# All five engines keep the written order in both attention stages, and the planner's estimate follows

## The chip, the core and the metric

The kernel runs on one core of a Trainium2 chip. The metric is device time in microseconds (us), the median of three runs. The engines are TensorE (PE; its weight loads are listed apart as PEld), VectorE (DVE), ScalarE (ACT), GpSimd (POOL) and SyncE (SP), which issues the DMAs.

## What is computed

One inference step of a two-layer decoder trunk, for a prompt of 1024 tokens and 8 samples of 4 new tokens each (32 more columns, 1056 in all), with model width 1024.

- Layer 0: stick-breaking attention with 8 heads of 64 beside a gated linear recurrence (RG-LRU); both outputs go through one output projection. Then an MLP with squared ReLU and width 4096.
- Layer 1: dilated sliding-window attention with 16 heads, three window branches merged by their softmax denominators, with a relative bias. Then the same kind of MLP, and a final RMS norm.
- The samples attend to a paged cache (layer 0) and to a window buffer (layer 1).

```python
z = einsum('bqhd,bkhd->bhqk', qb, k) * scale + bias          # layer 0
sp = where(mask, softplus(z), 0)
rest = cumsum(sp, reverse=True) - sp
w = where(mask, exp(log_sigmoid(z) - rest), 0)
o = einsum('bhqk,bkhd->bqhd', w, v)
...
p = exp(logits - m)                                           # layer 1, each branch
o = einsum('gnhqk,gnkhd->gnqhd', p, vb) / p.sum(-1)
```

## The kernel before

Activations lie transposed (features on partitions). For precision every matmul operand is split into a high and a low part, and a product takes three matmuls (high by high, high by low, low by high; `mm3`). So each tile that PE reads is made by a pair: ACT copies the high part, DVE or POOL subtracts it for the low part.

**The stages in order:** RG-LRU of layer 0 (to about 212 us), attention of layer 0 (212 to 688), first MLP (688 to 1512, with the sample caches of layer 1 prepared beside it), attention of layer 1 (1512 to 2266), last MLP.

**Inside an attention stage** heads are handled in pairs (4 pairs in layer 0, 8 in layer 1). Python generators each emit a piece of work and yield what they wait for: `heads` (scores, transposes, weighted values), `projections` (q, k and v of the next pair, 24 matmuls of 352 columns for each third of a tile, in two PSUM accumulators `mm`), `sb_samples` or `dl_samples`, and `early_out` (the first part of the output projection) beside the last pairs. `interleave` (L934) picks the next piece among those whose inputs the planner holds to be ready, by fixed weights. Each call of `interleave` covers one pair. `split_pair` (L732), called before it, plans the eight splits of the new pair (four of q, four of k) with `after`, 2000 columns apart: each is an ACT copy, then on DVE a second copy (q) or a subtraction (k), then for q a subtraction on POOL; in layer 1 two of the four k subtractions are on POOL. `dl_samples` has 16 small ACT copies `qw` per pair.

**The planner** is `Clock` (L60). It counts in columns (2400 to a us) and holds for each tile when it is written and last read. `Timed` (L128) wraps the engines' calls and prices each with a constant plus nanoseconds per element; `passed` (L189) does so for PE. An engine in `order` is counted first in, first out; for the others `fit` (L105) puts an operation into the first hole after its inputs are there, also ahead of operations that were emitted earlier. A `Later` (made by `after`, L259) is emitted when PE's planned time reaches its due time; if its inputs are planned over 200 columns late, it is put off (`events`, L194). A weight tile's split is such a `Later`, due 14000 columns after its load was emitted (`load` in `projections`, L709). So the planner's estimate sets the order of emission of every engine, PE and the DMA queue included.

**The order in which the engines really run** is fixed when the program is built. `manual` (L955) names the engines that keep the order of emission, before the change PE, SP and POOL. For ACT and DVE the framework's scheduler makes the order: by its own estimate of durations it lets an operation that it holds to be ready pass one that waits. In the first MLP (`first_mlp`, L1254) all five engines keep the order of emission already. On the chip each engine then works through its list.

All operations of DVE, ACT, POOL and SP show line L138 (the wrapper), matmuls L209, transposes L215. Tiles: `u` are work tiles (transposed weights, high and low), `tr`, `mm`, `pv` PSUM tiles, `f` the scan's tile, `sa` and `sb` scores, `mx` row maxima and sums, `qa`, `ka` (first head of a pair), `qb`, `kb` (second head) split queries and keys, `ql` the low queries, `ws` raw weights, `w` split weights.

Of the kernel before, what the change touches and what calls it, by code (L numbers as in the profile page):

```python
# [12 lines left out]
R = mybir.dt.float32r  # L13
# [3 lines left out]
PSUM = bass.MemoryType.PSUM  # L17
# [3 lines left out]
SEQ = 1024  # L21
NS = 32
NT = SEQ + NS
CW = NT // 3
# [12 lines left out]
def f32(ap):  # L37
    return ap.bitcast(F)
# [21 lines left out]
class Clock:  # L60
# [12 lines left out]
    def __getattr__(self, n):  # L73
        return getattr(self.nc, n)
# [51 lines left out]


class Timed:  # L128
    NS = {"scalar": (100, 0.82), "vector": (70, 1.04), "gpsimd": (100, 2.2), "sync": (0, 0)}

    def __init__(self, clock, e, engine):
        self.clock, self.e, self.engine = clock, e, engine
# [1 line left out]
    def __getattr__(self, n):  # L134
        f = getattr(self.engine, n)

        def call(*args, **kw):
            r = f(*args, **kw)  # L138
            aps = [a for a in list(args) + list(kw.values()) if hasattr(a, "name") and hasattr(a, "shape")]
            outs = aps[:1] + ([kw["accum_out"]] if "accum_out" in kw else [])  # L140
            if self.e == "sync":
                o = aps[0] if aps[0].space != DRAM else aps[1]
                cost = int(np.prod(o.shape)) * 4 / 360 * 2.4
                outs = [a for a in outs if a.space != DRAM]
                ins = [a for a in aps[1:] if a.space != DRAM]
            else:
                a, b = Timed.NS[self.e]
                cost = (a + b * int(np.prod(aps[0].shape[1:]))) * 2.4
                ins = aps[1:]
            self.clock.run(self.e, cost, outs, ins)  # L150
            return r
        call.timed = True
        return call
# [18 lines left out]
class Trunk:  # L172
# [35 lines left out]
    def mm(self, out, w, x, start, stop):  # L208
        self.nc.tensor.matmul(out, w, x, start=start, stop=stop)  # L209
        n = int(np.prod(x.shape[1:]))  # L210
        m = int(np.prod(w.shape[1:]))
        self.passed(max(n, 2 * m) if x.dtype == R else max(4 * n, 4 * m), [out], [w, x])

    def tr(self, out, x, ident):
        self.nc.tensor.transpose(out, x, ident)  # L215
# [126 lines left out]
    def mm3(self, ps, terms):  # L342
        n = len(terms)
        for i, (wh, wl, xh, xl) in enumerate(terms):
            mm = self.mm
            mm(ps, wh, xh, start=i == 0, stop=False)
            mm(ps, wh, xl, start=False, stop=False)
            mm(ps, wl, xh, start=False, stop=i == n - 1)
            if i < n - 1:
                yield 0, 0  # L350
# [31 lines left out]
    def norm_finish(self, st):  # L382
# [4 lines left out]
        def sums():  # L387
            ps = self.tr_ps([128, 9])
            for t in range(9):
                n = 128 if t < 8 else NS  # L390
                self.mm(ps[:n, t:t + 1], acc[:, t * 128:t * 128 + n], self.ones[:, 0:1],
# [6 lines left out]
    def spread_rstd(self, r, rstd):  # L398

        nc = self.nc  # L400
        for c in range(3):
            pb = self.tr_ps([128, 384])
            w = 0
            for t in range(3 * c, 3 * c + 3):
                n = 128 if t < 8 else NS
                self.mm(pb[:, w:w + n], r[:n, t:t + 1].to_broadcast([n, 128]),
# [4 lines left out]
    def rsqrt(self, ps, last=True):  # L411
# [6 lines left out]
        if last:  # L418
            nc.vector.memset(m[:, k:], 1.0)
            nc.vector.tensor_scalar(m[:NS, k:], ps[:NS, k:], 1.0 / D, EPS, op0=OP.mult, op1=OP.add)  # L420
        nc.scalar.activation(t, m, AF.Sqrt)
# [531 lines left out]
            e[2] += self.work - c0  # L953

    def manual(self):  # L955
        self.nc.order.add("gpsimd")
        return self.tc.manual_schedule(engines={mybir.EngineType.PE, mybir.EngineType.SP, mybir.EngineType.Pool, })

    def heads(self, pairs, q_step, k_step, v_step, T, far, done, lag):

# [293 lines left out]
    def first_mlp(self, st, rstd, w1, w2, h, nx):  # L1254
        nc, hp = self.nc, self.hp
        todo = self.caches(hp)
        raw, parts = {}, {}

        def load(u):
            g, x = divmod(u, 8)  # L1260
            if x < 4:
                c0 = (g * 4 + x) * 128
                raw[u] = self.raw_w(w1[:, :, c0:c0 + 128], 8, 128)
            else:
                raw[u] = self.raw_w(w2[:, g * 4:g * 4 + 4, (x - 4) * 256:(x - 3) * 256], 4, 256)

        def cut(u, half):
            if u >= 64:
                return
            if half == 0:  # L1270
                parts[u] = self.parts_w(*raw[u].shape[1:], *((hp, 2) if u % 3 == 2 else ()))
            (a, b), kb = parts[u], raw[u].shape[1]
            c = slice(0, kb // 2) if half == 0 else slice(kb // 2, kb)
            nc.scalar.activation(a[:, c], raw[u][:, c], AF.Copy)
            if half:
                nc.gpsimd.tensor_sub(b, raw.pop(u), f32(a))

        load(0)
        load(1)
        cut(0, 0)  # L1280
        cut(0, 1)
        load(2)
        cut(1, 0)
        cut(1, 1)
        load(3)
        next(todo)
        with self.tc.manual_schedule(engines={getattr(mybir.EngineType, e) for e in
                                              ("PE", "SP", "Pool", "Activation", "DVE")}):
            for u in range(64):
                g, x = divmod(u, 8)  # L1290
                if u + 4 < 64:
                    load(u + 4)
                if x == 0:
                    th, tl = ([hp.tile([128, NT], R, name=self.nm(t), tag=t, bufs=4) for _ in range(4)]
                              for t in ("th", "tl"))
                w = parts.pop(u)
                n = 0
                if x < 4:
                    for c in range(3):
                        s = slice(c * CW, (c + 1) * CW)  # L1300
                        ps = self.mm_ps([128, CW])
                        for _ in self.mm3(ps, [(w[0][:, k], w[1][:, k], st["xh"][k][:, s], st["xl"][k][:, s])
                                               for k in range(8)]):
                            pass
                        for t in st["ready"]:
                            t.run()
                        t = hp.tile([128, CW], F, name=self.nm("t"), tag="t", bufs=3)
                        q = hp.tile([128, CW], F, name=self.nm("t2"), tag="t2", bufs=3)
                        nc.vector.scalar_tensor_tensor(t, ps, 0.0, rstd[:, s], op0=OP.max, op1=OP.mult)
                        nc.scalar.activation(q, t, AF.Square)  # L1310
                        nc.scalar.activation(th[x][:, s], q, AF.Copy)
                        next(todo, None)
                        nc.vector.tensor_sub(tl[x][:, s], q, f32(th[x][:, s]))
                        next(todo, None)
                        if c < 2:
                            cut(u + 2, c)
                    continue
                step = self.norm_done(h, self.g[:, 1], nx) if g == 7 else None

                def done(m, s):  # L1320
                    nonlocal n
                    if step:
                        step(m, s)
                        if s.stop == NT:
                            nc.sync.dma_start(self.hs[1][m], h[m])
                    next(todo, None)
                    if n in (1, 3):
                        cut(u + 2, n // 2)
                    n += 1
                if u == 63:  # L1330
                    w1c = self.i["w_in_c"][0].rearrange("(k p) f -> p k f", p=128)
                    first = self.load_w(w1c[:, :, :128], 8, 128)
                    nx["w"] = first, self.after(14000, self.split_w, *first, need=first[:1], made=first[1:])
                m = 2 * (x - 4)
                for _ in self.contract(w, (m, m + 1), range(4), th, tl, h, done):
                    pass
            for _ in todo:
                pass
        self.norm_finish(nx)
# [763 lines left out]
```

## Time and profile before

| | us |
|---|---|
| median of 3 runs (lowest, highest) | 3074.31 (3070.54, 3074.38) |
| profiled execution, its own time | 3073.03 |
| its span, first to last instruction | 3071.3 |
| PE busy | 2874.8 (94%) |
| DVE busy | 1711.0 (56%) |
| ACT busy | 1258.4 (41%) |
| POOL busy | 978.9 (32%) |

Busy time is a mean over stages with different limits, and a busy PE is not PE at its peak. The view by stretches of time gives, for each stretch, the busy time of every engine with its number of instructions, the granted PE clock (1.00 is 2.4 GHz) and the load of the DMA engines. The views of waits name, for each engine, what ended its idle time.

### The profile page before, as it was taken

The page shows a single profiled execution, that of the slowest core. Times are in us where ns is not written, and L with a number is a line of the kernel's source. Part 1 is how long each engine was busy: PE and PEld are TensorE (multiplying, and loading weights), DVE is VectorE, ACT ScalarE, POOL GpSimd, SP SyncE. Part 2 cuts the span into 40 slices and gives each one's busy share as a digit, 9 for nine tenths or more (in the row PEclk, how much of TensorE's full clock was granted, in tenths as well). Part 3 has the DMA queues.
Part 4 walks back from the last instruction along what each step waited for, and adds up shares of the span by engine and source line. Part 5 has one row for each costly group of instructions (what it writes and reads, how often), then busy time and mean ns, then how long its engine had stood idle before and what let it go on. Part 6 is the DMA issues. An engine that isn't in the chain of part 4 may idle for free.

```text
span 3071.3 us, 49475 instructions
## 1 busy us (share of the span) xinstructions
PE 2874.8 (94%) x18608; PEld 2757.7 (90%) x18608; DVE 1711.0 (56%) x3657; ACT 1258.4 (41%) x2505; POOL 978.9 (32%) x613
## 2 busy tenths in 40 slices
PE   7878889979999999999999989998989999999998
PEld 7778878849999999999988888897889999999998
DVE  6868887875444444433467777766673333333335
ACT  4446666654333333333344555544452222122222
POOL 2436552443333333332412222222231122121222
PEclk9889999979999999999999999998999999999999
DMA  5111127574877777761365544555631111111111
GB/s 171 42 44 34 42 86 222 166 240 133 256 246 250 251 253 251 258 206 42 120 190 187 191 148 160 188 170 191 220 119 49 48 49 42 49 43 48 49 35 64
DMA packets 366728, 426.18 MB, mean 139 GB/s; under 512 B 23878, under 2 KB 292822, under 8 KB 366488
## 3 DMA queue, kind: packets, MB, share of 16 engines
q1 hardware_dynamic: 366488, 423.01, 42.9%
q8 instruction: 147, 2.41, 0.3%
q14 instruction: 93, 0.76, 0.1%
HBM read 296.23 MB, written 126.17 MB: 138 GB/s over the span
## 4 chain that ended last, share of the span: by engine, by line
PE 63%; DVE 6%; DMA 4%; ACT 3%; issue 1%; SPq 0%; POOL 0%; ACTq 0%; DVEq 0%; POOLq 0%
PE mm L209 54%; PE tr L209 6%; DMA ws<-in_w_in_c_dram 3%; PE tr L215 2%; PE pv L209 1%; DVE sa L138 1%; DVE sb L138 1%; ACT w L138 1%; DVE u L138 1%; DVE tl L138 1%; SPq L138 0%; DVE ats L138 0%; ACT sb L138 0%; DVE mx L138 0%; ACT o L138 0%
## 5 line engine op out<-in xcount | busy, mean ns | idle before, releaser
L209 PE MATMUL mm<-xh,w 128*128 128x352 f32 x5184 | 1380.0, 333 | 14.5 <-DVE xr L138 7.4
L209 PEld LDWEIGHTS mm<-xh,w 128*128 128x128 f32 x5184 | 939.3, 192 | 24.4 <-DVE xr L138 8.6
L138 POOL TENSOR_TENSOR w<-ws,w 128x1024 fp32r<-128x1024 f32 (+1 forms) x188 | 460.6, 2450 | 1378.9 <-ACT w L138 1295.0
L209 PE MATMUL mm<-xl,w 128*128 128x352 f32 x2592 | 848.4, 327 | 2.8 <-DVE xl L138 2.8
L209 PE MATMUL mm<-th,w 128*128 128x352 f32 (+2 forms) x3072 | 742.5, 323 | 4.4 <-DVE h L138 4.4
L209 PEld LDWEIGHTS mm<-th,w 128*128 128x128 f32 x3072 | 533.1, 188 | 7.0 <-DVE h L138 6.4
L209 PEld LDWEIGHTS mm<-xl,w 128*128 128x128 f32 x2592 | 500.9, 193 | 7.7 <-DVE xl L138 3.1
L209 PE MATMUL mm<-tl,w 128*128 128x352 f32 (+2 forms) x1536 | 493.2, 321 | 0.0
L138 ACT ACTIVATE w<-ws 128x512 fp32r<-128x512 f32 (+1 forms) x376 | 220.4, 617 | 581.2 <-issue 266.7
L138 DVE TENSOR_TENSOR h<-mm,h 128x352 f32<-128x352 f32 (+2 forms) x384 | 200.4, 524 | 416.4 <-PE mm L209 415.7
L209 PEld LDWEIGHTS mm<-tl,w 128*128 128x128 f32 x1536 | 288.7, 188 | 0.0
L138 ACT ACTIVATE t<-t 128x352 f32<-128x352 f32 x192 | 95.1, 495 | 411.2 <-DVE t L138 411.2
L138 DVE TENSOR_TENSOR tl<-t,th 128x352 fp32r<-128x352 f32 x192 | 151.4, 789 | 192.5 <-ACT th L138 192.5
L138 DVE SCALAR_TENSOR_TENSOR t<-mm,rstd 128x352 f32<-128x352 f32 x192 | 100.4, 523 | 281.0 <-PE mm L209 276.5
L138 ACT ACTIVATE u<-tr 128x512 fp32r<-128x512 f32 (+5 forms) x362 | 188.0, 528 | 164.7 <-PE tr L215 139.1
L138 DVE TENSOR_TENSOR u<-tr,u 128x512 fp32r<-128x512 f32 (+3 forms) x272 | 164.7, 614 | 74.6 <-ACT u L138 71.0
L138 POOL TENSOR_TENSOR kvs<-raw,kvs 128x512 fp32r<-128x512 f32 x80 | 103.3, 1297 | 132.0 <-ACT kvs L138 60.4
L209 PE MATMUL pv<-u,v 128*128 128x256 f32 (+1 forms) x736 | 129.2, 294 | 13.1 <-DVE u L138 12.0
L209 PE MATMUL mm<-x,w 128*128 128x352 f32 x720 | 141.4, 334 | 0.1
L209 PEld LDWEIGHTS pv<-u,v 128*128 128x128 f32 x736 | 112.7, 200 | 16.7 <-DVE u L138 13.7
L209 PEld LDWEIGHTS mm<-x,w 128*128 128x128 f32 x720 | 118.2, 192 | 4.8 <-issue 1.0
L209 PE MATMUL tr<-u,x 128*64 128x128 f32 (+1 forms) x640 | 95.3, 284 | 24.0 <-DVE u L138 16.2
(286 smaller groups left out, 3796.5 us busy)
## 6 DMA issues: line engine op xcount, KB each, us to landing
kv<-kvs SPq DMA_DIRECT2D x160, 512.0 KB
U<-kv SPq DMA_DIRECT2D x160, 512.0 KB
ws<-in_w_ff_dram SPq DMA_DIRECT2D x126, 512.0 KB
raw<-in_cache_dil_k_dram SPq DMA_DIRECT2D x320, 64.0 KB
u<-in_cache_sb_k_dram SPq DMA_DIRECT2D x64, 256.0 KB
u<-in_cache_sb_v_dram SPq DMA_DIRECT2D x64, 256.0 KB
raw<-in_cache_dil_v_dram SPq DMA_DIRECT2D x64, 256.0 KB
out_dram<-u SPq DMA_DIRECT2D x48, 256.0 KB
```

The source lines that it names most:

```text
L138: r = f(*args, **kw)
L209: self.nc.tensor.matmul(out, w, x, start=start, stop=stop)
L215: self.nc.tensor.transpose(out, x, ident)
```

## The change

ACT and DVE join the engines that keep the order of emission in both attention stages (`manual`, through a new `in_order` that the first MLP uses too), and the planner counts them first in, first out. The prices in `Timed.NS` change, scans of 256 or more elements are priced twice as high per element, DVE operations with two large SBUF inputs 1.6 times, operations with an accumulator get 130 ns more, and a fast matmul counts 1.09 columns per column.

```diff
 class Timed:
-    NS = {"scalar": (100, 0.82), "vector": (70, 1.04), "gpsimd": (100, 2.2), "sync": (0, 0)}
+    NS = {"scalar": (170, 0.85), "vector": (150, 1.04), "gpsimd": (120, 2.4), "sync": (0, 0)}
...
                 a, b = Timed.NS[self.e]
-                cost = (a + b * int(np.prod(aps[0].shape[1:]))) * 2.4
                 ins = aps[1:]
+                c = int(np.prod(aps[0].shape[1:]))
+                if self.e == "vector" and c >= 256:
+                    big = [i for i in ins if i.space != PSUM and int(np.prod(i.shape[1:])) == c]
+                    b *= 2 if "scan" in n else 1.6 if len(big) > 1 else 1
+                cost = (a + b * c + (130 if "accum_out" in kw else 0)) * 2.4
...
     def mm(self, out, w, x, start, stop):
...
-        self.passed(max(n, 2 * m) if x.dtype == R else max(4 * n, 4 * m), [out], [w, x])
+        self.passed(max(1.09 * n, 2 * m) if x.dtype == R else max(4 * n, 4 * m), [out], [w, x])
...
     def manual(self):
-        self.nc.order.add("gpsimd")
-        return self.tc.manual_schedule(engines={mybir.EngineType.PE, mybir.EngineType.SP, mybir.EngineType.Pool, })
+        self.nc.order.update(("gpsimd", "scalar", "vector"))
+        return self.in_order()
+
+    def in_order(self):
+        return self.tc.manual_schedule(engines={getattr(mybir.EngineType, e) for e in
+                                                ("PE", "SP", "Pool", "Activation", "DVE")})
...
-        with self.tc.manual_schedule(engines={getattr(mybir.EngineType, e) for e in
-                                              ("PE", "SP", "Pool", "Activation", "DVE")}):
+        with self.in_order():
```

## Rows read from the trace of the kernel before

**Rows 1.** Busy time by stretch: us, each engine's busy us (instructions), PE clock, DMA share, GB/s.

```profile
212.00:640.00 428.00, 377.93 (x2750) 352.40 (x2751) 343.82 (x450) 271.40 (x530) 197.40 (x160) 0.94 0.37 115
640.00:688.00 48.00, 32.55 (x95) 14.07 (x94) 39.80 (x55) 26.34 (x46) 27.18 (x18) 0.72 0.79 255
688.00:1512.00 824.00, 813.29 (x5042) 810.66 (x5042) 353.96 (x625) 300.29 (x543) 304.07 (x162) 0.99 0.65 211
1512.00:2266.00 754.00, 694.89 (x4948) 647.40 (x4947) 521.83 (x1792) 360.53 (x863) 183.15 (x128) 0.96 0.54 173
```

**Rows 2.** PE's waits from 214 to 640 us: us, times, longest.

```profile
PE pv L209 <- DVE u L138: 11.7, 5, 3.8
PE tr L215 <- DVE u L138: 10.2, 6, 5.9
PE tr L209 <- DVE u L138: 10.0, 9, 2.1
PE tr L215 <- DVE sa L138: 4.3, 1, 4.3
```

**Rows 3.** PE's waits from 1512 to 2266 us, same columns.

```profile
PE tr L209 <- DVE u L138: 26.4, 14, 4.4
PE tr L215 <- DVE mx L138: 12.3, 18, 1.8
PE tr L209 <- DVE mx L138: 6.7, 5, 5.8
PE tr L215 <- DVE tl L138: 5.2, 7, 3.0
```

**Rows 4.** Timeline of all engines, 1721 to 1738 us: start, us, what [idle before <-releaser].

```profile
1721.47 0.39 SPq L138 DMA_DIRECT2D ws<-in_w_in_c_dram  x1
...
1732.59 1.15 ACT L138 ACTIVATE w<-ws 128x512 fp32r<-128x512 f32 x2 [3.80 <-DMA ws<-in_w_in_c_dram]
...
1735.19 0.16 DVE L138 RECIPROCAL mx<-mx 128x1 f32<-128x1 f32 x1 [4.42 <-ACT sa L138]
...
1737.04 0.69 PE L209 MATMUL tr<-ka,qa 128*128 128x384 f32 x1 [3.71 <-DVE u L138]
```

**Rows 5.** Timelines of PE near 1599 and 1996 us: first and last of six such waits.

```profile
1598.72 0.80 PE L209 MATMUL tr<-kb,qb 128*128 128x512 f32 x1 [3.85 <-DVE u L138]
...
1995.39 0.44 PE L209 MATMUL tr<-ka,qa 128*128 128x384 f32 x1 [4.42 <-DVE u L138]
```

**Rows 6.** DVE's groups by line and tile, 212 to 688 us: count | busy us, mean ns.

```profile
L138 DVE TENSOR_TENSOR_SCAN f<-f,ms 128x128 f32<-128x128 f32 (+3 forms) x64 | 92.4, 1446 | 10.1 <-ACT f L138 9.9
```

**Rows 7.** Timeline of PE, 440 to 456 us.

```profile
442.58 1.14 PE L215 MATMUL tr<-ident,k 128*128 128x128 f32 x9
...
454.36 1.11 PE L215 MATMUL tr<-ident,u 128*128 128x128 f32 x4 [5.87 <-DVE u L138]
```

**Rows 8.** Timeline of DVE, 440 to 460 us.

```profile
447.78 1.99 DVE L138 CAST qb<-qb 64x512 fp32r<-64x512 f32 x1
449.70 1.75 DVE L138 TENSOR_TENSOR kb<-k,kb 64x512 fp32r<-64x512 f32 x1
...
453.62 0.69 DVE L138 TENSOR_TENSOR u<-tr,u 128x512 fp32r<-128x512 f32 x1
```

**Rows 9.** Timeline of ACT, 409 to 420 us.

```profile
410.31 0.63 ACT L138 ACTIVATE qa<-q 64x512 fp32r<-64x512 f32 x1
```

**Rows 10.** Timeline of PE, 368 to 392 us: the boundary of the pair before.

```profile
368.22 0.60 PE L215 MATMUL tr<-ident,k 128*128 128x128 f32 x4
...
390.66 0.22 PE L209 MATMUL tr<-ka,qa 128*128 128x128 f32 x1
```

**Rows 11.** DVE's groups by shape, 212 to 688 us: the second head's splits.

```profile
L138 DVE CAST qb<-qb 64x512 fp32r<-64x512 f32 x8 | 10.7, 1334 | 0.2
L138 DVE TENSOR_TENSOR kb<-k,kb 64x512 fp32r<-64x512 f32 x8 | 10.1, 1268 | 0.3 <-ACT kb L138 0.2
```

**Rows 12.** DVE's groups by shape, 1512 to 2266 us: the splits of both heads.

```profile
L138 DVE CAST qb<-qb 64x512 fp32r<-64x512 f32 x16 | 14.2, 890 | 1.1 <-ACT qb L138 0.7
L138 DVE TENSOR_TENSOR kb<-k,kb 64x512 fp32r<-64x512 f32 x8 | 12.8, 1594 | 0.2
...
L138 DVE CAST qa<-qa 64x512 fp32r<-64x512 f32 x15 | 6.3, 419 | 0.3
L138 DVE TENSOR_TENSOR ka<-k,ka 64x512 fp32r<-64x512 f32 x8 | 5.5, 685 | 1.0 <-ACT ka L138 0.6
```

**Rows 13.** ACT's groups by shape, 1512 to 2266 us: the samples' small copies.

```profile
L138 ACT ACTIVATE qw<-qs 32x16 fp32r<-32x16 f32 x128 | 27.2, 212 | 5.2 <-POOL qw L138 3.6
```

**Rows 14.** All waits from 1512 to 2266 us: ACT on weight loads.

```profile
ACT w L138 <- DMA ws<-in_w_in_c_dram: 62.6, 15, 7.1
```

**Rows 15.** Timeline of PE, 440 to 456 us: distance of two projection matmuls in a row.

```profile
439.89 0.32 PE L209 MATMUL mm<-xl,w 128*128 128x352 f32 x1
440.05 0.32 PE L209 MATMUL mm<-xh,w 128*128 128x352 f32 x1
```

## The prediction

> **What bounds the kernel now.** I read the stretches first [rows 1]. The first MLP (688 to 1512 us), in which all five engines already keep the written order, leaves PE idle for 824 - 813.3 = 10.7 us, 1.3%. The two attention stages leave it idle for 50.1 + 15.5 us (212 to 640 and 640 to 688) and for 59.1 us (1512 to 2266): 125 us in 1230, 10%, and the granted clock is 0.94, 0.72 and 0.96 there against 0.99. So PE is the bound everywhere, and what a better order can win lies in these 125 us. DVE is the next engine: busy for 80% of 212 to 640, 83% of the tail, 69% of layer 1's attention, against 43% in the MLP.
>
> PE's waits [rows 2, 3] name DVE as the releaser, above all the tile `u`, whose low part DVE subtracts: 11.7 + 10.2 + 10.0 + 4.3 = 36.2 us in layer 0 and 26.4 + 12.3 + 6.7 + 5.2 = 50.6 us in layer 1 (the eight rows that matter).
>
> Two examples show what a wait is made of. At 454 us PE waits 5.87 us for a `u` [rows 7] that DVE subtracts only at 453.62, after it has copied `qb` (1.99 us) and subtracted `kb` (1.75) and two more splits [rows 8]: the splits of a later score pass ahead of what PE wants now. This is a wait of order. At 1737 us the chain is another: a weight load issued at 1721.47 is awaited by ACT until 1732.59 (3.80 us idle), behind it DVE waits 4.42 us for ACT's scores, and PE 3.71 us for DVE [rows 4]. This is a wait for a DMA, handed on. There are six such, from 1599 to 1995 us, the first 3.85 and the last 4.42 us [rows 5], 20.2 us together with 1.35, 3.71, 3.46 and 3.45 between them.
>
> **The change, part by part.**
>
> *Prices.* No instruction is added or removed on any engine; what changes is the order, on PE, POOL and SP too, since the planner's clock decides when each piece is emitted, loads and stores with it. The old prices hold DVE for lighter than it is. The 64 scans of layer 0 (eight of each length from 128 to 1024) took 92.4 us [rows 6]; old, 64 x 0.07 + 8 x 4608 x 1.04 ns = 42.8 us; new, 8 x (0.283 + 7 x 0.15 + 4480 x 2.08 ns) = 85.2 us. So the planner was 50 us short in a stage of 476, and sent PE to transposes whose operands were not there. A projection matmul follows the next after 0.16 us [rows 15]; 352 columns were 0.147 us and become 0.160. These edits cost nothing themselves; they act through the order below.
>
> *Gain: waits of order.* Of 36.2 + 50.6 us I take off the six DMA waits, 20.2: 66.6 us that a right estimate could fill with projection or `early_out` matmuls. Bounds: none (the waits only move) to all (the MLP's 1.3% idle says that an in-order stage can run nearly dense). I take six tenths, 40 us: nearer to the MLP, but its DVE is half as loaded. The tail from 640 us has no other PE work left, so I count nothing there.
>
> *Cost: the splits of a pair come together.* The scheduler lets the first head's splits of the next pair pass, as soon as the last score that reads the old `qa` is done: ACT copies `qa` at 410.31 [rows 9], while the pair only begins with the transposes of k at 442.58 [rows 7]. In the written order `split_pair` emits all eight after the pair has begun. There are 3 such boundaries in layer 0 and 7 in layer 1. Moved to each: in layer 0 two casts and two subtractions on DVE, in layer 1 two casts and one subtraction (the other is on POOL), and four copies on ACT.
>
> Which price? The first head's splits, alone, take 419 and 685 ns in layer 1; the second head's, in a bunch with POOL's subtractions, 890 and 1594 [rows 12]. In the bunch, then: layer 0 2 x 1.334 + 2 x 1.268 = 5.2 us [rows 11], layer 1 2 x 0.890 + 1.594 = 3.4 us, in all 3 x 5.2 + 7 x 3.4 = 39 us of DVE. At the price of first-head splits the layer 1 part would be 7 x (2 x 0.419 + 0.685) = 10.7 instead of 23.6 us, and the sum 26 us. I take the bunch. (The Trainium skill, SBUF — State Buffer, section Who interferes with whom, says that a DVE copy or cast in a two-port mode, and a DVE instruction with two SBUF inputs, block against a GpSimd instruction that reads SBUF; by this rule the dearer price holds, as POOL's own subtractions stand in the same bunch, and the trace agrees: 419 against 890 ns.)
>
> How much of it reaches PE? From the transposes of k to the first score of the new pair there are 22 us (368.22 to 390.66 [rows 10]), and PE has projections for them, but only two `mm` accumulators before DVE must empty one: 2 x 24 x 0.16 = 7.7 us of cover. The whole row of DVE's splits is 4 x 1.334 + 4 x 1.268 = 10.4 us in layer 0, 2.7 over the cover; in layer 1 it is 4 x 0.890 + 2 x 1.594 = 6.7 us, under it. So 3 x 2.7 = 8 us; bounds 0 and the whole 39 (cover gone).
>
> *Cost: ACT blocked by small copies.* The 128 `qw` copies take 27.2 us, 3.4 per pair [rows 13]. Written, they stand right behind the sample split whose second half is DVE's, so ACT waits there for DVE, and the score copies behind it wait too. Bounds 0 to 27 us; I take a quarter, 7 us, since projections cover it at most pair starts.
>
> *Weight loads, no change taken.* ACT waits 62.6 us for them in layer 1 [rows 14]. The split is emitted 14000 columns, 5.8 us, after its load, and the load at 1721.47 was awaited until 1732.59, 11.1 us [rows 4]: in the written order ACT comes there 5.3 us too early, now 3.8. The DMA's price in the planner does not change. Bounds: the 20.2 us freed, or 20.2 x (5.3/3.8 - 1) = 8 us more.
>
> *Clock.* Short of full by 0.06, 0.28 and 0.04 over 428, 48 and 754 us: 69 us, partly the echo of the waits. I take none back; it widens the range downward.
>
> **Sum:** -40 + 8 + 7 = -25 us. The profiled execution took 3073.03 us, so 3048; it lies 1.3 us under the median of 3074.31, so I forecast **3049**.
>
> **The rivals.** *Slower: the bunch stands uncovered.* Place: the ten pair boundaries. Price: all 39 us and the 7 for `qw`, while a third of the order waits is won (22): 3074 + 24 = 3098. It decides once DVE's row there, with the evacuation of `mm` queued behind it, outlasts 7.7 us; in layer 1 it is 1 us short of that. For it speaks that DVE now has the boundary's waits already with half the splits [rows 7, 8]; against it, that the planner counts these splits in order and sees PE's work come late.
>
> *No change: the waits only move.* DVE is busy for 80% of layer 0's stage; a wait filled early leaves less projection work to fill a later one, and gains and new blocks cancel: 3074. The change would also do nothing much if the scheduler's order were near the written one already; against that stand the 32 us by which `qa` goes ahead [rows 7, 9].
>
> *Much faster.* All 66.6 us go and the bunch is covered: 3074 - 67 = 3007; some clock comes back too. For it speaks the MLP's dense order, against it the DVE load.
>
> **How the numbers follow.** About 0.2%, 6 us, can be told from no change here. Chances: the forecast 0.46, much faster 0.14, no change 0.13, slower 0.27. So faster 0.60, same 0.13, slower 0.27. The range reaches from the much faster case, 3007, to the slower one, 3098, widened to 3005 and 3100; beyond it lie the freed DMA waits and clock below, all costs with no gain above, together 0.2. The forecast's own range is 3025 to 3068.
>
> **What would show it.** Right: PE's waits for DVE's `u` fall from 36 and 51 us by half or more while ACT's wait for weight loads stays near 63 us; `qa` copies stand behind the transposes of k, not 32 us before; the casts of `qa` in layer 1 take nearer 890 than 419 ns; DVE's idle time before `mm` evacuations stays short. Wrong: new PE waits on `mm` evacuations (k, v, q) at pair starts, ACT idle before `qw` or before weight splits by tens of us, or a longer tail after 640 us.

## The result, and the profile after

The changed kernel took **3094.47 us** (median of 4 runs, 3092.82 to 3098.87), the kernel before it 3072.43 (3067.77 to 3074.38) beside it: ratio 1.0076, 95% interval 1.0059 to 1.0094. It is slower by 22 us by the medians (23 by the ratio), where 3049 was forecast. The profiled execution took 3093.83 us, with a span of 3092.1.

Busy time by stretch in the changed kernel (columns as in [rows 1]):

```profile
212.00:640.00 428.00, 378.76 (x2760) 351.16 (x2759) 336.00 (x453) 274.81 (x534) 202.15 (x157) 0.94 0.38 119
640.00:688.00 48.00, 33.70 (x85) 13.20 (x84) 40.61 (x49) 23.35 (x41) 26.53 (x17) 0.71 0.73 230
688.00:1512.00 824.00, 813.17 (x5037) 810.47 (x5037) 353.90 (x625) 297.95 (x542) 305.15 (x162) 0.99 0.65 210
1512.00:2266.00 754.00, 694.94 (x4862) 647.89 (x4861) 513.44 (x1756) 351.12 (x846) 182.94 (x126) 0.94 0.54 170
```

Up to 1512 us the two kernels stand level. In layer 1's attention the same 754 us hold 4862 PE instructions instead of 4948, and the clock is 0.94 instead of 0.96. The loss is there. The stage itself, from its first transposes of k to the first transposes after its last pair, is one stretch in each kernel; before, then after:

```profile
1535.50:2264.00 728.50, 669.39 (x4795) 621.90 (x4794) 510.86 (x1777) 348.99 (x833) 170.82 (x118) 0.96 0.55 177
```

```profile
1535.10:2282.50 747.40, 683.70 (x4793) 635.60 (x4791) 522.11 (x1788) 355.54 (x856) 175.60 (x121) 0.93 0.55 173
```

The stage is 18.9 us longer. PE's idle time (stretch minus busy) grew from 59.1 to 63.7 us only; its busy time, for the same work, grew by 14.3. So three quarters of the loss are PE working at a lower granted clock, 0.93 against 0.96. By pairs, the first seven took 615.4 us before and 616.4 after; the last went from 113.1 to 131.0. (That the first seven stand level is a gain and a loss that cancel, as the run `f1` shows below.)

PE's waits after (us in total, times, longest), from 214 to 640 us and from 1512 to 2285 us, as in [rows 2, 3]:

```profile
PE tr L213 <- DVE u L138: 15.8, 13, 7.2
PE mm L213 <- DVE q L138: 10.8, 3, 5.6
PE pv L213 <- DVE u L138: 8.5, 2, 4.9
...
PE tr L213 <- ACT qw L138: 25.0, 17, 3.7
PE tr L213 <- DVE mx L138: 9.9, 9, 4.3
PE tr L219 <- DVE sb L138: 9.0, 9, 2.2
PE mm L213 <- DVE q L138: 5.4, 5, 2.2
PE tr L213 <- DVE u L138: 2.8, 1, 2.8
```

In layer 1 the waits for `u` are nearly gone (26.4 to 2.8 us), and a new one has their size: the first sample products of a pair (`tr<-U,qw`) wait for ACT's small copies `qw`. Where those copies run is seen in the view of the tile `qs` around one boundary (each row: number, ns least/median/most, first and last start; the rows stand by busy time, and the chain runs `qs` on ACT, `qs` on DVE, `qw` on ACT). Before, the pair begins at 1781.3 us:

```profile
L138 ACT ACTIVATE qw<-qs x16: 198/213/216, 1724.9 to 1734.2; 32x16 fp32r<-32x16 f32 x16
L138 ACT ACTIVATE qs<-q x1: 229/229/229, 1723.7 to 1723.7; 128x32 fp32r<-128x32 f32 x1
L138 DVE TENSOR_TENSOR qs<-q,qs x1: 153/153/153, 1724.3 to 1724.3; 128x32 fp32r<-128x32 f32 x1
```

After, it begins at 1782.4:

```profile
L138 ACT ACTIVATE qw<-qs x16: 211/213/216, 1785.8 to 1789.2; 32x16 fp32r<-32x16 f32 x16
...
L138 ACT ACTIVATE qs<-q x1: 239/239/239, 1779.6 to 1779.6; 128x32 fp32r<-128x32 f32 x1
L138 DVE TENSOR_TENSOR qs<-q,qs x1: 183/183/183, 1785.6 to 1785.6; 128x32 fp32r<-128x32 f32 x1
```

The scheduler had let this chain over two engines run 47 to 58 us ahead of this boundary (at the other boundaries the copies `qw` started 34 to 73 us ahead). In the written order its last two links run 3 to 7 us behind it, and only seven PE instructions stand between the boundary and the product that reads `qw`. PE's timeline there, after (start, us, what [idle before <-releaser]):

```profile
1781.89 0.32 PE L213 MATMUL mm<-xh,w 128*128 128x352 f32 x1
...
1786.72 0.50 PE L213 MATMUL tr<-U,qw 128*128 128x256 f32 x2 [3.20 <-ACT qw L138]
...
1792.28 0.50 PE L213 MATMUL mm<-xl,w 128*128 128x352 f32 x1
```

Around that boundary, the stretches of both kernels, before and then after:

```profile
1781.30:1787.00 5.70, 5.54 (x40) 5.18 (x41) 5.51 (x18) 5.31 (x11) 5.49 (x4) 1.00 0.80 201
1787.00:1795.00 8.00, 8.00 (x64) 7.95 (x63) 7.01 (x9) 2.35 (x5) 4.23 (x3) 1.00 1.01 373
```

```profile
1783.50:1787.60 4.10, 0.51 (x3) 0.30 (x2) 2.43 (x13) 1.71 (x8) 0.46 (x2) 1.00 0.66 207
1787.60:1795.00 7.40, 6.92 (x27) 6.29 (x28) 2.88 (x4) 7.20 (x16) 3.14 (x2) 0.54 0.47 164
```

After PE was busy for 0.51 of 4.10 us, the next 7.40 us ran at a granted clock of 0.54, so nearly all at the lower level, 1.2 GHz, and held 27 instructions where 8.00 us before held 64 (partly others). So this short wait cost more than its own length.

The last pair has one more. SP's waits from 2140 to 2190 us, and SP's timeline from 2167 us (start, us, what), both after:

```profile
SPq L138 <- POOL ql L138: 12.2, 1, 12.2
```

```profile
2167.21 0.32 SPq L138 DMA_DIRECT2D q<-hs  x1
...
2168.16 1.98 SPq L138 DMA_DIRECT2D U<-kv  x4
```

The load `q<-hs` overwrites the pair's q tile, so it waits until POOL has made its last low query from it (3.4 us before the change, 12.2 now). POOL waits for the splits, which are all at the boundary now. Behind that load on SP stand the loads `U<-kv` that PE's sample products read. Before, two were issued 2 us and four more 7 us behind the boundary; now the first comes 17 us behind it. SP's timeline before:

```profile
2152.53 0.88 SPq L138 DMA_DIRECT2D U<-kv  x2
...
2157.76 2.12 SPq L138 DMA_DIRECT2D U<-kv  x4
```

### The profile page after: what moved, and what is told of

Read it like the earlier page. It is cut to its first block, busy times and chain, and to the rows that moved or that the text cites. A ratio compares the mean times of both kernels' runs of the same rounds, so it can differ in the third digit from the quotient of the medians.

```text
span 3092.1 us, 49498 instructions
## 1 busy us (share of the span) xinstructions
PE 2888.0 (93%) x18608; PEld 2766.0 (89%) x18608; DVE 1711.1 (55%) x3657; ACT 1257.4 (41%) x2505; POOL 993.2 (32%) x613
## 4 chain that ended last, share of the span: by engine, by line
PE 75%; DVE 11%; ACT 5%; issue 4%; DMA 3%; POOL 2%; SPq 0%; ACTq 0%; DVEq 0%; POOLq 0%
PE mm L213 60%; PE tr L213 8%; PE tr L219 4%; PE pv L213 3%; DVE sb L138 1%; DVE u L138 1%; DVE sa L138 1%; ACT qw L138 1%; DVE w L138 1%; ACT u L138 1%; ACT w L138 1%; DVE xl L138 1%; DVE f L138 1%; DVE qa L138 0%; DMA u<-in_cache_sb_v_dram 0%
## 5 line engine op out<-in xcount | busy, mean ns | idle before, releaser
L213 PE MATMUL mm<-xh,w 128*128 128x352 f32 x5184 | 1338.4, 330 | 31.4 <-DVE q L138 17.2
L213 PEld LDWEIGHTS mm<-xh,w 128*128 128x128 f32 x5184 | 929.9, 192 | 41.0 <-DVE q L138 19.5
L213 PE MATMUL pv<-u,v 128*128 128x256 f32 (+1 forms) x736 | 136.0, 304 | 8.6 <-DVE u L138 8.5
```

## The experiments

Each was run with the kernel before on the same chip; that took 3072.96 to 3075.80 us there, 1 to 3 us more than beside the changed kernel. Differences below are of medians; by the ratios the repairs give 4 to 6 us more. So 33 us, say, stand for 33 to 38. Three theories stood at the start: A, the work that comes together behind each pair's boundary costs; B, the new durations give PE a worse order; C, each engine in order costs a little everywhere.

### The two halves of the change, and the two stages

New durations without the written order, in both stages (`f1`); the written order with the old durations (`f2`); all of it but the order in layer 0 alone (`f3`) and in layer 1 alone (`f4`).

```diff
 f1: manual() as before the change, Timed and mm as after it
 f2: Timed and mm as before, manual() as after it
-                with self.manual():
+                with self.manual(ordered):   # f3: True in layer 0, False in layer 1; f4: the reverse
```

> The new prices alone, with ACT and DVE again left to the framework's scheduler and counted by first hole. Theory A (what costs is the written order at pair starts: all splits and the small copies come in one bunch behind the boundary): the loss is gone, 3055 to 3075 us, the last pair of layer 1 back near 113 us from 131. Theory B (the new prices give PE a worse order, since the weights of interleave were set with the old ones): the loss stays, about 3090. Theory C (ACT and DVE block a little everywhere in the written order): as A, 3055 to 3075.

> The written order with the old prices. Theory A: still slower than before, 3090 to 3115, with the last pair of layer 1 near 131 us and SP waiting about 12 us for POOL's ql there. Theory B: near before, 3072. Theory C: slower than the change, 3100 or more, since waits can no longer be foreseen.

> The written order in layer 0's attention alone, new prices in both. Theory A: layer 0 gained 2 us up to its MLP in the changed kernel's trace, the loss sits in layer 1, so 3068 to 3076. Theory C: half of the loss, about 3083.

> The written order in layer 1's attention alone, new prices in both. Theory A: nearly the whole loss, 3088 to 3098, last pair near 131 us. Theory C: half of it, about 3083. Theory B: as the change, 3094, whatever the order.

| | us | ratio to before, 95% |
|---|---|---|
| f1, durations alone | 3037.28 | 0.9870 to 0.9903 |
| f2, order alone | 3102.30 | 1.0075 to 1.0108 |
| f3, order in layer 0 | 3043.20 | 0.9883 to 0.9916 |
| f4, order in layer 1 | 3096.12 | 1.0058 to 1.0092 |

The durations alone give 36 us, so B falls as long as the scheduler orders ACT and DVE, and f1 beats both kernels. The order, which here means the engines' written order and the planner's count of it together, costs 59 us in layer 1. In layer 0 it costs 6 us by the medians, but the intervals of f1 and f3 overlap, and on top of layer 1's order it costs nothing (f4 against the changed kernel).

Not all was as expected. f1 and f3 lie below every time that a theory gave them, since the theories took the durations to be worth less. f4 is as A had it. In f2 the time fits A and C, but the last pair took 125.2 us and SP waited 6.2 us for `ql`, where A had some 131 and 12.

The stage of layer 1 with the durations alone, and PE's largest waits in it:

```profile
1532.60:2221.70 689.10, 652.60 (x4793) 613.28 (x4792) 515.77 (x1777) 348.61 (x831) 169.84 (x116) 0.98 0.58 186
```

```profile
PE tr L219 <- DVE mx L138: 14.5, 5, 5.3
PE tr L219 <- DVE tl L138: 5.9, 1, 5.9
PE tr L213 <- DVE u L138: 3.4, 8, 0.6
```

It is 39.4 us shorter than before: 22.6 of PE's idle time (59.1 to 36.5) and 16.8 of its busy time, at a clock of 0.98. So the gain came in layer 1, and two fifths of it are PE working faster at a higher clock. The idle time went at one place: PE's waits for `u` fell from 26.4 us [rows 3] to 3.4, none over 0.6, and with them went all six waits of 20.2 us together that hung on weight loads [rows 4, 5]. The other waits of [rows 3], 30 us, only fell to 25. ACT still waits for those loads, 34.1 us instead of 62.6 [rows 14]; why no such wait reaches PE any more is not shown.

By pairs, the first seven took 577.7 us and the last 111.5. So against f1 the changed kernel loses 38.7 us in its first seven pairs and 19.5 in the last; against the kernel before, the first loss is hidden by the gain.

### Three repairs of the changed kernel

The planner waits for `qs` and `qw` (`m1`); the last load behind its splits (`m2`); the first head's four splits of the next pair during the current one, as in [rows 9], in both layers (`m3`); all three (`m4`).

```diff
# m1, dl_samples
+            yield 0, [pp["qs"]]
             qs = f32(pp["qs"])
...
-            yield 0, [TR]
+            yield 0, [TR, qw]
# m2, early_out
                 yield None
+                yield 0, list(pp["split"])
+                for t in pp["split"] + pp["split_s"]:
+                    t.run()
+                yield 0, [pp["q32"].name]
                 resid(m)
# m3, heads: split_pair then leaves these four out
+                    if h and g and "v32" in pairs[p + 1] and "split" not in pairs[p + 1]:
+                        self.split_pair(pairs[p + 1], T, far, True)
```

> The changed kernel, with two more things that the planner waits for in layer 1's sample scores: the planned end of VectorE's low part qs before the qw copies of ScalarE are emitted, and the planned end of those copies before the first product that reads them. Theory A (the loss of the written order sits in a few waits at the pair boundaries, this one first: PE waits 25.0 us for qw in 17 gaps): the wait falls under 8 us and the time to 3065 to 3080. Theory C (every engine in order costs a little everywhere): the gap moves to the next instruction, the time stays within 6 us of the changed kernel's 3094.

> The changed kernel, where the last pair's load q<-hs in layer 1 is emitted only after the planned end of the splits that read the tile that it overwrites, so that the loads U<-kv behind it on SP are not held. Theory A (the last pair's 131 us against 113 come from SP's queue, which waits 12.2 us there for POOL's ql): that wait falls under 4 us, the last pair to some 118 us, the time to 3080 to 3088. Theory C: the last pair stays over 126 us and the time within 6 us of 3094.

> The changed kernel, where the four splits of the first head (two q, two k) of the next pair are emitted during the second head of the current one, as they ran in the kernel before, in both layers. Theory A (the bunch of eight behind the k transposes is what costs): pairs 0 to 6 of layer 1 fall from 85 to some 82 us, the three waits of PE for DVE's q behind the bunch in layer 0 go, and the time falls to 3070 to 3085. Theory C: within 6 us of 3094, since what is emitted earlier blocks other work earlier.

> The three edits together. Theory A: the parts add, 3040 to 3055, near the 3037 that the new durations gave without the written order. Theory C: 3085 or more.

- m1: 3075.09 (0.9991 to 1.0011), 19 us back. PE's wait for `qw` fell to 5.2 us. Of the 20.6 us by which the stage became shorter, 17.8 are PE's busy time, at a clock of 0.96; its idle time nearly stayed (60.9 us). So most of what came back is clock. A wait for ACT's `v` came up, so C has its part. The stage's row and that wait:

```profile
1535.40:2262.20 726.80, 665.90 (x4794) 624.96 (x4792) 504.32 (x1788) 357.22 (x856) 173.93 (x121) 0.96 0.57 178
```

```profile
PE tr L213 <- ACT v L138: 21.6, 6, 5.7
```

- m2: 3086.67 (1.0023 to 1.0049), 8 us back. SP's 12.2 us are gone, and the last pair took 121.7 us instead of 131.0 (118 was expected).
- m3: 3100.58 (1.0059 to 1.0093), nothing back. The first seven pairs took 631.0 us instead of 616.4, PE's waits for `sb` rose from 9.0 to 17.4 us and those for `u` from 2.8 to 11.1. A's first form, that the bunch of splits costs, falls in layer 1. In layer 0 PE's waits for DVE's `q`, which were to go, only fell from 10.8 to 8.6 us.
- m4: 3066.45 (0.9945 to 0.9985), 28 us back, which is m1 and m2 together (27) and nothing for m3; 3040 to 3055 was missed, and C's 3085 too.

### One engine alone, and the last load without the written order

```diff
-        self.nc.order.add("gpsimd")
+        self.nc.order.update(("gpsimd",) + e)   # n1: e = ("vector",), n2: ("scalar",), layer 1 only
# n3: f1 with the edit of m2
```

> The new durations, layer 0 left to the scheduler; in layer 1 VectorE keeps the written order, ScalarE does not. Theory S (it is ScalarE's order that costs: the qw copies stand behind other work there): 3037 to 3047, PE's wait for qw under 8 us, the granted clock of layer 1's stage near the 0.98 of the durations alone. Theory V (it is VectorE's, the busier of the two, 522 of 747 us: the qs part and the sums for the max stand behind the bunch of splits): 3075 to 3096, the clock at 0.93 to 0.95.

> The same with ScalarE in the written order in layer 1 and VectorE not. Theory S: 3075 to 3096, PE's wait for qw 20 us or more. Theory V: 3037 to 3050, that wait under 8 us.

> The new durations without the written order, and the last pair's load q<-hs emitted behind the splits that read its tile (SP waits 7.0 us there for POOL's ql in the kernel with the durations alone). If this queue costs in that kernel too: 3030 to 3035, the last pair of layer 1 at some 106 us instead of 111. If it is covered there by other waits (5.9 us for tl): 3036 to 3039.

n1 took 3096.72 us (1.0050 to 1.0091), n2 3095.94 (1.0049 to 1.0088): either engine alone loses all 59 us, so neither S nor V holds. The tiles `qs` and `qw` show the part of it that both have. With VectorE alone in order, at the boundary of 1783.0 us:

```profile
L138 ACT ACTIVATE qw<-qs x16: 198/213/215, 1788.1 to 1791.5; 32x16 fp32r<-32x16 f32 x16
...
L138 ACT ACTIVATE qs<-q x1: 231/231/231, 1730.5 to 1730.5; 128x32 fp32r<-128x32 f32 x1
L138 DVE TENSOR_TENSOR qs<-q,qs x1: 180/180/180, 1786.2 to 1786.2; 128x32 fp32r<-128x32 f32 x1
```

With ScalarE alone, at 1782.7:

```profile
L138 ACT ACTIVATE qw<-qs x16: 211/213/216, 1785.7 to 1789.1; 32x16 fp32r<-32x16 f32 x16
...
L138 ACT ACTIVATE qs<-q x1: 222/222/222, 1779.9 to 1779.9; 128x32 fp32r<-128x32 f32 x1
L138 DVE TENSOR_TENSOR qs<-q,qs x1: 177/177/177, 1785.5 to 1785.5; 128x32 fp32r<-128x32 f32 x1
```

The chain goes ACT, DVE, ACT, PE. A free ACT has its first link done 52 us ahead and then has to wait for DVE's. With a free DVE, ACT's first link comes only 2.8 us ahead of the boundary, and DVE's 5.6 us behind that, after work on the scores. One engine in order puts the last two links behind the boundary: PE waits 30.6 us for `qw` in n1 and 22.9 in n2. That both lose just the same 59 us is chance in part, since the sums are made up differently: the first seven pairs and the last took 628.9 and 118.8 us in n1, 620.8 and 130.3 in n2.

n3 took 3033.13 us (0.9851 to 0.9891), the least of all kernels. Against f1 (0.9870 to 0.9903) the intervals overlap: SP's wait for `ql` is gone there too, but the last pair is 110.3 us against 111.5, not 106. What the load costs without the written order is not settled.

### Order and estimate apart, and the chain moved ahead

`p1`: in layer 1 only the planner's estimate counts ACT and DVE in order, the scheduler keeps them free. `p2`: the reverse. `m5`: the changed kernel, with the next pair's `qs` and `qw` written during the current pair's last sample products. `m6`: m5 with m2.

```diff
# p1: nc.order has scalar and vector, manual_schedule has PE, SP, Pool; p2: nc.order lacks them, in_order()
# m5, dl_samples, in the loop over b of the values
+                    nx = pairs[p + 1] if p + 1 < len(pairs) else {}
+                    if "k32" in nx and "qs" not in nx:
+                        low(nx)          # qs: ScalarE's copy and VectorE's subtraction
+                    elif "qs" in nx and "spread" not in nx:
+                        yield 0, [nx["qs"]]
+                        spread(nx)       # the 16 qw copies and POOL's two
```

> The new durations, layer 0 as in the kernel with the durations alone. In layer 1 the scheduler keeps its freedom with VectorE and ScalarE, and only the estimate counts the two in order, so that PE's order follows from it. Theory W (the written order itself costs: the chain of ScalarE's qs, VectorE's qs and ScalarE's qw runs behind each pair's boundary, and either engine alone in order puts it there): 3037 to 3047, PE's wait for qw under 8 us. Theory E (the estimate in order gives PE a worse order): 3075 to 3096.

> The reverse: both engines keep the written order in layer 1, and the estimate counts them as free, as in the kernel before. Theory W: 3085 to 3100, PE's wait for qw 20 us or more. Theory E: 3037 to 3050.

> The changed kernel, where the sample part of the next pair's q is split and its 16 qw copies are written during the last products of the current pair's samples in layer 1, as the scheduler ran them in the kernel before (30 to 70 us ahead of the boundary). Theory W, with this chain as the largest part of the loss: PE's wait for qw under 4 us, no gap of 3 us at the boundaries, the granted clock of the stage back from 0.93 to 0.96 or more, 3060 to 3075. If the eight splits behind the boundary cost as much as the chain: the gap goes over to them (PE waits for mm evacuations or for splits), 3080 to 3094.

> The same, and the last pair's load q<-hs behind the splits that read its tile. If the two parts add: 7 to 9 us less than the run before it, the last pair at some 115 us. If the chain and the load waited for the same thing: within 3 us of it.

With the new durations and layer 0 left to the scheduler, layer 1 is now measured four ways:

| layer 1 | estimate free | estimate in order |
|---|---|---|
| scheduler orders ACT, DVE | 3037.3 (f1, 0.9870 to 0.9903) | 3062.4 (p1, 0.9937 to 0.9973) |
| written order | 3084.3 (p2, 1.0020 to 1.0049) | 3096.1 (f4, 1.0058 to 1.0092) |

Both halves cost: the written order 47 or 34 us, the estimate in order 25 or 12 (by the ratios 45 and 37, 21 and 13). PE waits for `qw` in p2 (25.9 us) and not in p1, as theory W has it, but p1 missed W's time by 15 us, and E's by 13: PE waits there for DVE's `mx` instead.

```profile
PE tr L219 <- DVE mx L138: 15.8, 10, 5.3
PE tr L213 <- DVE u L138: 7.1, 12, 2.2
PE tr L213 <- DVE mx L138: 6.9, 5, 3.8
```

These three sum to 29.8 us, against 19.3 for the same three in f1 (14.5, 3.4 and 1.4); that is 10 of the 25 us. Why an estimate in order should give PE the worse order even where the engines keep that order (p2 against f4) is not shown by these runs.

m5 took **3061.57** us (0.9940 to 0.9967): 33 us of the loss are this chain (with the two copies that POOL makes of `qs`, which were moved too). At the boundary of 1772.4 us it runs 40 us ahead; its copies there, then the stage's row and PE's largest waits:

```profile
L138 ACT ACTIVATE qw<-qs x16: 200/213/215, 1729.2 to 1732.5; 32x16 fp32r<-32x16 f32 x16
```

```profile
1539.10:2259.20 720.10, 671.34 (x4793) 631.39 (x4791) 525.21 (x1788) 355.92 (x857) 173.12 (x121) 0.95 0.56 180
```

```profile
PE mm L213 <- DVE q L138: 12.3, 6, 3.2
PE tr L219 <- DVE sb L138: 10.5, 7, 2.3
```

As theory W has it, the wait for `qw` is gone but for 0.8 us; the clock, 0.95, is short of the 0.96 expected; PE's idle time fell from 63.7 to 48.8 us and its busy time from 683.7 to 671.3. (This profiled execution took 3070.56 us, 9 above the kernel's median, so it shows rather less than the whole.) m6 took 3053.34 us (0.9903 to 0.9952), 8 less. The intervals of m5 and m6 overlap a little, but the traces show where the 8 us lie: the first seven pairs are level (595.5 and 595.4 us), and the last went from 124.6 to 116.5. So the load adds.

In m5 the largest wait is for `mm` evacuations, 12.3 us, so the bunch was tried once more with the chain gone: m6 with the edit of m3 (`m7`).

> The qw copies ahead, the last load behind its splits, and the first head's splits of the next pair ahead as well (alone these gave nothing, while the qw chain stood at the same boundary). If the eight splits at the boundary are what is left of the loss (PE waits 9 to 12 us for mm evacuations behind them): 3040 to 3048, those waits under 5 us. If they are covered: within 4 us of 3053.

It took 3066.45 us (0.9959 to 0.9981), 13 more than m6. The waits for `mm` evacuations went, as wanted, and larger ones came:

```profile
PE tr L219 <- DVE sb L138: 21.0, 14, 3.4
PE tr L213 <- DVE u L138: 12.5, 6, 4.7
```

So of the two places that were tried for the four splits, behind the boundary is the better one. That they take DVE's time from the scores when they stand ahead is how the new waits read; it was not tested apart.

## Why the prediction was wrong

**Gain from a right estimate, -40: near in size for the durations alone, by luck, and not kept in the written order.** Without the order the durations give 36 us, 39.4 of them in layer 1's stage, with 3 more ahead of it and 6 given back behind it. But only 22.6 of the 39.4 are idle time; the rest is clock, for which nothing had been taken. And the idle time is that of the six waits on weight loads, 20.2 us, which the prediction took off and put at no change. Of the 66.6 us of other waits, from which it took its 40, little went: layer 1's 30 us fell to 25 in f1, and the three waits for `u` of layer 0 [rows 2], 31.9 us, to 29.9 in f1 and 24.3 in the changed kernel. With the order the gain is not kept: the changed kernel against f2, the old durations in the written order, is 8 us better, with overlapping intervals. The waits for `u` did fall by more than half in layer 1, as foreseen, and that was no sign of a faster stage.

**The bunch of splits, +8: work and price right, the wait only in part.** The splits in the changed kernel, 1512 to 2285 us, against [rows 12]:

```profile
L138 DVE CAST qa<-qa 64x512 fp32r<-64x512 f32 x16 | 15.5, 968 | 22.9 <-ACT qa L138 22.6
...
L138 DVE TENSOR_TENSOR kb<-k,kb 64x512 fp32r<-64x512 f32 x8 | 15.1, 1887 | 0.7
...
L138 DVE TENSOR_TENSOR ka<-k,ka 64x512 fp32r<-64x512 f32 x8 | 8.9, 1118 | 12.5 <-ACT ka L138 12.4
```

The first head's cast went from 419 to 968 ns in the mean, its subtraction from 685 to 1118. The mean of the casts mixes two durations: taken one by one, nine of the sixteen took 0.42 us and seven 1.66 to 1.71, and each of the seven ran beside an instruction of POOL almost from end to end; seven of the nine touched one too, so standing beside one is not enough. (The rule cited from the Trainium skill, SBUF — State Buffer, Who interferes with whom, agrees.) In layer 0 PE's waits for DVE's `q` are 10.8 us in three gaps, near the 8 of the forecast, but not where it put them: the longest, 5.6 us, stands at the first pair, which has no pair before it, and one of 4.55 at the third. In layer 1, put at nothing, such waits are 5.4 us in the changed kernel and 12.3 in m5. Moving the first head's splits ahead gained nothing (m3), and with the chain gone it cost 13 us (m7). The rival "the bunch stands uncovered" named the right place, the boundary, and nearly the right time, 3098, but not the right work.

**ACT blocked by `qw`, +7, bounds 0 to 27: this step failed.** Moving the chain ahead gave 33 us back, more than the upper bound. The step priced the copies by ACT's own busy time, 27.2 us [rows 13], and took projections for cover. It did not look where the chain stood before, up to 58 us ahead of the boundary, nor what PE does next: the product that reads `qw` has four to seven PE instructions ahead of it behind the boundary, and only when the planner is made to wait (m1) does PE take other work first. The step saw that ACT waits for DVE's half of the sample split, but not that this chain had run ahead and that one engine in order is enough to hold it. The prediction had named the sign, ACT idle before `qw` by tens of us: it is 28.0 us, in the view below.

**Clock, none taken: wrong.** 14.3 of the 18.9 us by which the stage grew are busy time at a lower clock, and the gain of f1 is to two fifths clock. A term at nothing in both directions hid three quarters of the loss and two fifths of that gain.

**Weight loads, no change taken: wrong.** The six waits of PE that hung on them, 20.2 us, are gone without the written order (f1) and with it: PE's waits for `u` in layer 1's stage are 3.4 and 2.8 us. ACT's own waits for the loads were 62.6 us [rows 14]. In the changed kernel, from 1512 to 2285 us, and then before, from 1512 to 2266, the view of all waits has

```profile
ACT u L138 <- PE tr L219: 165.4, 97, 10.1
...
ACT qw L138 <- DVE qs L138: 28.0, 7, 5.8
...
ACT w L138 <- DMA ws<-in_w_in_c_dram: 7.1, 2, 5.3
```

```profile
ACT u L138 <- PE tr L215: 71.0, 62, 3.4
```

In order, ACT waits more for PE's transposes and for `qs`. That it therefore comes to the weight splits later, and finds the loads there, is a reading; it was not tested apart from the planner's new times for the loads.

**Not foreseen: SP.** The prediction said that the splits are moved, but did not follow who waits for their last reader: POOL's `ql`, behind it SP's `q<-hs`, behind that the `U` loads. 8 us (m2, and again from m5 to m6).

**What stays open.** From m6 (3053) to f1 (3037) 16 us are left (13 by the ratios). Up to 6 may be layer 0's order. The rest, in layer 1, was not traced to one place: in the traces the stage of m6 is 23 us longer than that of f1, 18 of them in the first seven pairs. The effect of the estimate in order (25 or 12 us) is measured but not explained.

## What to carry to other kernels

Before taking an engine from a scheduler, list what the scheduler runs far ahead of its place in the text, tile by tile, and follow each chain to the PE instruction that reads it; a chain over two engines was lost here as soon as one of them was in order. Price such a wait with the stretch of low clock that follows it, and look at every queue that waits for the last reader of a moved piece, the DMA queue too. Try durations and order apart: here the first were worth 36 us, and the second took all of it and some 20 more.

## What the runs showed of the hardware

After the 4.10 us from 1783.5 in which PE was busy for 0.51, it worked for most of 7.4 us at the lower level of the clock; within that stretch a matmul of 352 columns took 0.50 us (at 1792.28) instead of 0.32 (at 1781.89). Not every gap has this behind it: in m1 one of 3.05 us ahead of 1551.35 was followed by a granted clock of 1.00. Idle time alone does not tell what is lost: m1 kept 60.9 us of it against 63.7, and took 17.8 us less PE busy time. Read in steps of 0.5 us of the profile, layer 1's stage spent some 60 us at the lower level in the kernel before, 99 in the changed one, 61 in m1 and 34 in f1 (an estimate from these rows).

The first head's casts on DVE, all of 64x512, took either 0.42 us or 1.66 to 1.71 in layer 1 of the changed kernel, and the slow ones all ran beside an instruction of POOL.
